# Priority for the weight sums and parts of the t2 and t3 products in all early pairs of a SwiGLU

## The chip, the cores and the metric

One core of one Trainium2 chip runs the whole program. The metric is device time in microseconds (us), the median of 3 runs. Matrix products run on TensorE (PE, with PEld for its weight loads), elementwise work on VectorE (DVE) and ScalarE (ACT), a little on GpSimd (POOL); SyncE (SP) issues nearly all DMAs.

## The reference, cut to what matters

Two request groups (512 and 256 tokens, handled as 768 columns) go through two layers. Each layer has a half SwiGLU, a mixer, and another half SwiGLU, so there are four SwiGLUs, which this text counts from 1 to 4:

```python
def swiglu(h, wg, wu, wd):
    return (jax.nn.silu(h @ wg) * (h @ wu)) @ wd

def even_layer(x, ...):
    x = x + 0.5 * swiglu(rmsnorm(x, f1_n), f1_g, f1_u, f1_d)
    x = x + mixer_ab(rmsnorm(x, mix_n), ...)
    x = x + 0.5 * swiglu(rmsnorm(x, f2_n), f2_g, f2_u, f2_d)
    return x
```

The odd layer has the same form with another mixer. D_MODEL is 1024, D_FF 2816, everything is float32.

## The kernel before, in words

**Precision.** An fp32 operand is split into a high part (rounded to a format TensorE multiplies fast) and a low remainder, and a product is three passes: high by high, low by high, high by low (`mm3`, L152). For weights, `wsplit` writes the high part `whi` with an ACT cast (L122) and the low part `wlo` with a DVE subtraction (L123).

**Seven products in place of eight.** The gate and up products of a SwiGLU are made by a Strassen-like scheme over 2 x 2 blocks: the columns' halves (384 each), the two halves of the 1024 rows, and two tiles of 128 hidden features. 22 tiles of hidden features make 11 pairs (`pair(p)`). Each pair and each of gate and up needs the products with the operands b11, b21, t2, t3, n4, t1 and b22. The products with t2, t3, t1 and b22 take sums of weight blocks, made on DVE at L727 (`sums`): s1 and s2 for t2, s3 for t3, s1 again for t1, and s4, which is formed in place over s2, for b22.

**Early pairs.** The first four pairs (`EARLY = 4`) start before the operands and the norm's scale are all there. They run b11 and b21 first, in an interleaved order (`ORDERS`), with their results copied by ACT out of PSUM (`p1`, L602), reload their weights, and then run `settle`: for t2, t3, n4, t1, b22, each for gate and up, the weights' parts (`parts`) are written one product ahead, and the first parts of the next pair are entered during the current one. In pair 0's `settle` PE also meets the matmuls that spread the norm's scale of the second half of the columns (`ps_aux<-diag,onesr`); what they read, `diag`, is made on DVE at the end of a chain of small 128x3 operations (L317 to L308). The products t1 and b22 accumulate in one PSUM bank: after t1 DVE adds the bank to u3 (`add`, L577), and only then may b22 go on in it.

**What sets the order.** PE's order is the order of the code. On the other engines a scheduler orders the instructions when the program is built, by the order of the code, dependences and its own estimates; inside `high_priority()` it takes an instruction earlier. On the chip each engine then takes its list in order. A weight load (512 KB, SP, `raw<-in_w`) waits for one of four buffers, that is, for the last reader of an older weight. Before the change one thing in `parts` had priority: t2's sums and parts, and of one pair alone, pair 0 in the first SwiGLU and pair 3 in the others (`urgent`, L484 and L548).

Of the kernel before, what the change touches and what calls it, by code (L numbers as in the profile page):

```python
# [44 lines left out]
EARLY = 4  # L45
# [10 lines left out]
class Trunk:  # L56
# [421 lines left out]
    def ffn(self, pre):  # L478
# [2 lines left out]
            self.fw = self.open("work", self.other(self.guards["comb"][1]))  # L481
        rt, scales = self.acc, self.scales
        mixed = bool(self.unfed)
        urgent = 0 if self.first else EARLY - 1  # L484
        hs = {}

        etile = self.etile
# [38 lines left out]
        def pair(p):  # L526
# [16 lines left out]
            def sums(n, name):  # L543
                return self.sums(a[n, 1, 1], a[n, 1, 2], a[n, 2, 1], a[n, 2, 2], s, n, name)

            def parts(n, b):
                name = {"t2": "s2", "t3": "s3", "t1": "s1", "b22": "s4"}.get(b)
                with self.tc.high_priority() if b == "t2" and p == urgent else nullcontext():  # L548
                    return self.wsplit(sums(n, name) if name else a[n, 2, 2], nc.vector)

            def product(n, w, b, key, start, st=None):
# [89 lines left out]
            def entry():  # L641
                load((0, 1))
                return parts("gate", "t2")

            def settle(st):

                todo = [(n, b) for b in ("t2", "t3", "n4", "t1", "b22") for n in names]
                key = {"t1": "Z", "b22": "Z"}
                for i, (n, b) in enumerate(todo):
                    now, st = st, None  # L650
                    if i + 1 < len(todo):
                        st = parts(*todo[i + 1])
                    elif p + 1 < EARLY and (p % 2 or not p):
                        entered[p + 1] = entries[p + 1]()
                    if b == "t2":
                        begin(n, e[n, "p1"])
                    product(n, None, b, key.get(b, "Y"), b == "t1", now)
                    if b in ("t2", "t3"):
                        keep(b.replace("t", "u"), "Y", n)
                    elif b == "n4":  # L660
                        next(steps, None)
                    else:
                        add("Z", n, "u3" if b == "t1" else "u2")
                    if n == "up":
                        if b == "n4":
                            hidden(1, 0, bank["Y", "gate"], bank["Y", "up"])
                        elif b == "t1":
                            hidden(1, 1, e["gate", "u3"], e["up", "u3"])
                        elif b == "b22":
                            hidden(0, 1, e["gate", "u2"], e["up", "u2"])  # L670
# [1135 lines left out]
```

## Time and profile before

| what | value |
|---|---|
| median of 3 runs | 2600.09 us (2599.57 to 2600.18) |
| the profiled execution, first to last instruction (its own time) | 2599.3 us |
| what lies around that span, against the median | 0.8 us |
| PE busy | 2557.6 us (98%), 15114 matmuls |
| DVE busy | 2250.6 us (87%), 4691 instructions |
| ACT busy | 1364.7 us (53%), 2869 instructions |

PE is nearly full, so the time is the sum of its matmuls plus its waits. A row of the waits view names who waited, for what, how long in total, how often, and the longest. A timeline row is start, duration, engine, line, operation, output and inputs, and, in brackets, the engine's idle time before it and what ended it. Buffer numbers are left out of names there. DVE and ACT overlap the end of one instruction with the next, so what one costs in a full queue is the distance of two starts, not its duration.

### The profile page before, as it was taken

The numbers are of one execution on the slowest core, as the hardware profiler recorded it, in microseconds if no ns is written. First come the engines' busy times: TensorE is split into PE (matmuls) and PEld (weight loads), VectorE is DVE, ScalarE is ACT, GpSimd is POOL, SyncE is SP. The second block draws the span as 40 slices with busy tenths as digits, with TensorE's granted clock in tenths as the row PEclk, the third lists the DMA queues.
The fourth block names the chain that finished last, engine by engine and source line by source line (L and its number), as shares of the span: only waits on it lengthen the run. The fifth ranks groups of instructions, "written<-read, shape, count | busy, mean of one in ns | idle before, by whom it ended". The sixth has DMA issues, their size and how long they took to land.

```text
span 2599.3 us, 41191 instructions
## 1 busy us (share of the span) xinstructions
PE 2557.6 (98%) x15114; PEld 2489.5 (96%) x15114; DVE 2250.6 (87%) x4691; ACT 1364.7 (53%) x2869; POOL 113.4 (4%) x191
## 2 busy tenths in 40 slices
PE   8999999999999999999999999999999999999998
PEld 8999999988899999999999999998898999999997
DVE  7998898889779989889999889886777699888897
ACT  7554454556656544445655445454545475444543
POOL 0000000000120000000000000001222210000000
PEclk9999999999999999999999999999999999999999
DMA  6333222421133322223222222242221332222222
GB/s 217 112 106 101 71 82 66 139 84 51 55 106 98 98 66 74 74 65 98 84 95 79 68 76 71 65 145 64 64 64 40 106 98 90 82 68 79 69 67 77
DMA packets 86202, 221.88 MB, mean 85 GB/s; under 512 B 20464, under 2 KB 33264, under 8 KB 86000
## 3 DMA queue, kind: packets, MB, share of 16 engines
q1 hardware_dynamic: 85712, 218.96, 26.9%
q8 instruction: 119, 1.95, 0.3%
q14 instruction: 83, 0.68, 0.1%
q10 hardware_dynamic: 288, 0.29, 0.0%
HBM read 209.78 MB, written 15.07 MB: 87 GB/s over the span
## 4 chain that ended last, share of the span: by engine, by line
PE 66%; DVE 5%; ACT 1%; issue 1%; DMA 1%; DVEq 0%; ACTq 0%; SPq 0%
PE ps_mm L152 40%; PE ps_aux L152 25%; PE ps_aux L156 1%; DVE wlo L123 1%; DMA raw<-in_w 1%; ACT p L1089 0%; DVE tmp L415 0%; DVE p L1099 0%; DVE p L1083 0%; DVE s L727 0%; DMA mf<-in_nmask 0%; DVE u L589 0%; DVE u L577 0%; DVE acc L235 0%; DVE tmp L393 0%
## 5 line engine op out<-in xcount | busy, mean ns | idle before, releaser
L122 ACT CAST whi<-s 128x512 fp32r<-128x512 f32 x496 | 304.9, 621 | 404.7 <-DVE s L727 178.6
L122 ACT CAST whi<-raw 128x512 fp32r<-128x512 f32 x504 | 305.4, 619 | 215.6 <-PE ps_mm L152 87.5
L123 DVE TENSOR_TENSOR wlo<-s,whi 128x512 fp32r<-128x512 f32 x496 | 338.3, 686 | 53.3 <-ACT whi L122 48.2
L123 DVE TENSOR_TENSOR wlo<-raw,whi 128x512 fp32r<-128x512 f32 x468 | 320.7, 693 | 15.2 <-ACT whi L122 11.3
L152 PE MATMUL ps_mm<-db,whi 128*128 128x384 f32 x864 | 219.3, 334 | 0.4 <-DVE sg L586 0.4
L152 PE MATMUL ps_aux<-dt,whi 128*128 128x384 f32 x864 | 219.2, 334 | 0.0
L152 PEld LDWEIGHTS ps_mm<-db,whi 128*128 128x128 f32 x864 | 155.9, 188 | 0.8 <-DVE sg L586 0.8
L152 PEld LDWEIGHTS ps_aux<-dt,whi 128*128 128x128 f32 x864 | 156.0, 188 | 0.0
L152 PE MATMUL ps_mm<-xh,whi 128*128 128x512 f32 (+1 forms) x416 | 146.2, 352 | 0.0
L152 PE MATMUL ps_aux<-dt,wlo 128*128 128x384 f32 x432 | 144.4, 334 | 1.4 <-DVE wlo L123 1.4
L152 PE MATMUL ps_mm<-db,wlo 128*128 128x384 f32 x432 | 144.3, 334 | 0.0
L152 PE MATMUL ps_mm<-xl,whi 128*128 128x512 f32 (+1 forms) x416 | 141.4, 340 | 0.0
L152 PE MATMUL ps_mm<-xh,wlo 128*128 128x512 f32 (+1 forms) x416 | 141.2, 339 | 0.0
L727 DVE TENSOR_TENSOR s<-raw 128x512 f32<-128x512 f32 x124 | 85.0, 687 | 20.9 <-DMA raw<-in_w 20.9
L577 DVE TENSOR_TENSOR u<-ps_aux,u 128x384 f32<-128x384 f32 x176 | 97.3, 553 | 5.6 <-PE ps_aux L152 5.2
L727 DVE TENSOR_TENSOR s<-raw,raw 128x512 f32<-128x512 f32 x124 | 84.2, 687 | 20.4 <-DMA raw<-in_w 20.2
L152 PE MATMUL ps_aux<-dh,whi 128*128 128x384 f32 x384 | 97.5, 334 | 0.0
L779 DVE TENSOR_TENSOR x<-ps_aux,x 128x384 f32<-128x384 f32 x160 | 84.9, 552 | 13.6 <-PE ps_aux L152 13.6
L1089 ACT ACTIVATE p<-p,st 128x256 f32<-128x256 f32 (+3 forms) x144 | 68.9, 480 | 49.4 <-DVE st L1087 49.3
L572 ACT COPY u<-ps_mm 128x384 f32<-128x384 f32 x176 | 83.5, 475 | 16.7 <-PE ps_mm L152 16.6
L779 DVE TENSOR_TENSOR x<-ps_mm,x 128x384 f32<-128x384 f32 x160 | 86.4, 552 | 5.8 <-PE ps_mm L152 5.5
L152 PEld LDWEIGHTS ps_mm<-xh,whi 128*128 128x128 f32 x416 | 79.8, 192 | 9.3 <-issue 0.9
(515 smaller groups left out, 8088.5 us busy)
## 6 DMA issues: line engine op xcount, KB each, us to landing
raw<-in_w SPq DMA_DIRECT2D x346, 512.0 KB, 3.7
xdm<-x SPq DMA_DIRECT2D x16, 384.0 KB, 2.4
x<-in_x SPq DMA_DIRECT2D x16, 192.0 KB, 4.6
tok<-in_xt SPq DMA_DIRECT2D x12, 256.0 KB, 5.2
xold<-xdm SPq DMA_DIRECT2D x8, 384.0 KB, 3.1
x<-xdm SPq DMA_DIRECT2D x8, 384.0 KB, 4.6
out_y<-y SPq DMA_DIRECT2D x8, 384.0 KB, 2.7
tab<-skew SPq DMA_DIRECT2D x8, 256.0 KB, 6.3
```

Of the source, the lines that this page charges most:

```text
L122: nc.scalar.copy(hi, src)
L123: (eng or nc.gpsimd).tensor_tensor(out=lo, in0=src, in1=hi.bitcast(F32), op=ALU.subtract)
L152: self.nc.tensor.matmul(out, lhsT=lhsT, rhs=rhs, start=start, stop=stop, **kw)
L156: self.nc.tensor.transpose(out, src, self.ident)
L572: nc.scalar.copy(e[n, out], bank[key, n])
L577: nc.vector.tensor_tensor(out=t, in0=bank[key, n], in1=t, op=ALU.add)
L727: f = lambda o, x, y, op: self.nc.vector.tensor_tensor(out=o, in0=x, in1=y, op=op)
L779: nc.vector.tensor_tensor(out=o, in0=ps, in1=o, op=ALU.add)
L1089: ins = nc.scalar.activation(outs[i], outs[i], AF.Exp, bias=nm[:, i : i + 1], accum_out=sm[:, i : i + 1])
```

## The change

`urgent` goes, and the sums and parts of t2 and of t3 get priority in each of the four early pairs, in each of the four SwiGLUs.

```diff
@@ -481,7 +481,6 @@
         rt, scales = self.acc, self.scales
         mixed = bool(self.unfed)
-        urgent = 0 if self.first else EARLY - 1
         hs = {}
@@ -545,7 +544,7 @@
             def parts(n, b):
                 name = {"t2": "s2", "t3": "s3", "t1": "s1", "b22": "s4"}.get(b)
-                with self.tc.high_priority() if b == "t2" and p == urgent else nullcontext():
+                with self.tc.high_priority() if b in ("t2", "t3") and p < EARLY else nullcontext():
                     return self.wsplit(sums(n, name) if name else a[n, 2, 2], nc.vector)
```

No instruction is added or removed. The order on PE and POOL stays; that on DVE, ACT and SP changes in the first 50 to 250 us of each SwiGLU and nowhere else. One line is gone, so the changed program's lines from L485 on are one lower (L727 is L726 there).

Place 1 is DVE in SwiGLU 2, pair 0, where the chain of the norm's scale ends in `diag`. wlo617 is the low part for t3, wlo618 and wlo620 are those for n4, wlo621 that for t1; t12l and t13l are low parts of the operand t1. Before:

```order
L295 CAST yh_9084<-sm_8914 128x3
L408 SCALAR_TENSOR_TENSOR t11l_8202<-tmp_8587,gains_99,t11h_8201 128x384
L296 TENSOR_TENSOR yl_9085<-sm_8914,yh_9084 128x3
L308 TENSOR_SCALAR diag_9088<-ident_84,yh_9084 128x128 x3
L123 TENSOR_TENSOR wlo617_9055<-s3_9052,whi617_9054 128x512
L123 TENSOR_TENSOR wlo618_9075<-raw115_8987,whi618_9074 128x512
L408 SCALAR_TENSOR_TENSOR t12l_8204<-tmp_8589,gains_99,t12h_8203 128x384
L123 TENSOR_TENSOR wlo620_9111<-raw117_8991,whi620_9110 128x512
L408 SCALAR_TENSOR_TENSOR t13l_8206<-tmp_8591,gains_99,t13h_8205 128x384
L123 TENSOR_TENSOR wlo621_9129<-s1_8993,whi621_9128 128x512
```

With the change:

```order
L123 TENSOR_TENSOR wlo618_9075<-raw115_8987,whi618_9074 128x512
L326 TENSOR_TENSOR sm_8914<-sm_8914 128x3
L408 SCALAR_TENSOR_TENSOR t12l_8204<-tmp_8589,gains_99,t12h_8203 128x384
L327 TENSOR_TENSOR sm_8914<-sm_8914 128x3
L123 TENSOR_TENSOR wlo620_9111<-raw117_8991,whi620_9110 128x512
L328 SCALAR_TENSOR_TENSOR sm_8914<-sm_8914 128x3
L408 SCALAR_TENSOR_TENSOR t13l_8206<-tmp_8591,gains_99,t13h_8205 128x384
L295 CAST yh_9084<-sm_8914 128x3
L123 TENSOR_TENSOR wlo621_9129<-s1_8993,whi621_9128 128x512
L296 TENSOR_TENSOR yl_9085<-sm_8914,yh_9084 128x3
L308 TENSOR_SCALAR diag_9088<-ident_84,yh_9084 128x128 x3
```

Six instructions that stood behind `diag` now stand ahead of it (the five here and wlo617), and none that stood ahead has gone behind. SwiGLU 4 shows the same six.

Place 2 is DVE in SwiGLU 2, end of pair 0 and start of pair 1. u3_9108 is the L577 addition of `up` that frees the bank for the b22 product of `up`; raw118 to raw121 are pair 1's weights. Before:

```order
L577 TENSOR_TENSOR u3_9072<-ps_aux623_9156,u3_9072 128x384
L727 TENSOR_TENSOR s1_9225<-raw119_9219 128x512
L586 TENSOR_TENSOR u3_9072<-u3_9072,acc_8239 128x384
L727 TENSOR_TENSOR s2_9227<-s1_9225,raw118_9217 128x512
L577 TENSOR_TENSOR u3_9108<-ps_aux625_9177,u3_9108 128x384
L727 TENSOR_TENSOR s1_9250<-raw121_9223 128x512
```

With the change:

```order
L576 TENSOR_TENSOR u3_9072<-ps_aux623_9156,u3_9072 128x384
L726 TENSOR_TENSOR s2_9227<-raw118_9217,s2_9227 128x512
L726 TENSOR_TENSOR s1_9250<-raw121_9223 128x512
L585 TENSOR_TENSOR u3_9072<-u3_9072,acc_8239 128x384
L726 TENSOR_TENSOR s2_9252<-s1_9250,raw120_9221 128x512
L726 TENSOR_TENSOR s3_9278<-raw118_9217,raw119_9219 128x512
L726 TENSOR_TENSOR s3_9301<-raw120_9221,raw121_9223 128x512
L123 TENSOR_TENSOR wlo628_9255<-s2_9252,whi628_9254 128x512
L123 TENSOR_TENSOR wlo630_9281<-s3_9278,whi630_9280 128x512
L123 TENSOR_TENSOR wlo632_9304<-s3_9301,whi632_9303 128x512
L576 TENSOR_TENSOR u3_9108<-ps_aux625_9177,u3_9108 128x384
```

Nine more instructions stand ahead of u3_9108 than before, all 128x512: the eight here with L726 and L123, and wlo627 a few rows higher. They are the sums and parts of pair 1's t2 and t3 and, with the second s2_9227, the sum for its b22.

Place 3 is ACT in SwiGLU 3, where the result of the b11 product of `up`, pair 3, is copied out of bank ps_mm998 (p1_14318), before the b21 product may go on in it. whi1004 reads the sum s2_14386, which needs pair 0's last weight load. Before:

```order
L594 COPY ps_mm1007_14414<-p1_14013 128x384
L602 COPY p1_14318<-ps_mm998_14278 128x384
L122 CAST whi1004_14388<-s2_14386 128x512
L587 ACTIVATE sg_14320<-sg_14320 128x384
L587 ACTIVATE sg_14362<-sg_14362 128x384
```

With the change:

```order
L593 COPY ps_mm1007_14414<-p1_14013 128x384
L122 CAST whi1004_14388<-s2_14386 128x512
L601 COPY p1_14318<-ps_mm998_14278 128x384
L122 CAST whi1006_14410<-s3_14408 128x512
L586 ACTIVATE sg_14320<-sg_14320 128x384
```

The cast whi1004 has moved from behind the copy to ahead of it.

## Rows read from the trace of the kernel before

**Rows 1.** The page, part 1: busy time, share of the span, instructions.
```profile
PE 2557.6 (98%) x15114; PEld 2489.5 (96%) x15114; DVE 2250.6 (87%) x4691; ACT 1364.7 (53%) x2869; POOL 113.4 (4%) x191
```

**Rows 2.** PE's waits, 45 to 160 us (SwiGLU 1): who, for what: us, times, longest.
```profile
PE ps_mm L152 <- ACT whi L122: 4.1, 2, 2.2
PE ps_mm L152 <- DVE wlo L123: 2.3, 4, 0.8
```

**Rows 3.** PE's waits, 785 to 860 us (SwiGLU 2).
```profile
PE ps_mm L152 <- DVE wlo L123: 2.2, 4, 0.8
PE ps_mm L152 <- ACT whi L122: 1.2, 2, 0.9
```

**Rows 4.** PE's waits, 2112 to 2190 us (SwiGLU 4), those for high parts.
```profile
PE ps_mm L152 <- ACT whi L122: 1.2, 2, 1.0
```

**Rows 5.** Windows in SwiGLU 2, 3, 4: length, busy PE, PEld, DVE, ACT, POOL, clock, DMA.
```profile
785.00:809.90 24.90, 23.36 (x134) 22.39 (x133) 24.90 (x64) 18.30 (x42) 0.00 (x0) 1.00 0.30 85
785.00:831.00 46.00, 43.66 (x249) 42.17 (x248) 45.77 (x102) 27.80 (x61) 0.00 (x0) 1.00 0.30 92
1278.00:1310.00 32.00, 32.00 (x186) 31.51 (x185) 28.70 (x67) 17.30 (x37) 0.00 (x0) 1.00 0.29 100
2112.00:2158.00 46.00, 43.67 (x248) 42.17 (x247) 45.76 (x102) 27.79 (x61) 0.00 (x0) 1.00 0.31 92
```

**Rows 6.** PE's timeline in SwiGLU 2, pair 0.
```profile
803.46 0.44 PE L152 MATMUL ps_mm<-t20h,whi 128*128 128x384 f32 x1 [0.95 <-ACT whi L122]
809.92 0.51 PE L152 MATMUL ps_aux<-diag,onesr 128*128 128x384 f32 x2
821.71 0.33 PE L152 MATMUL ps_aux<-b220h,whi 128*128 128x384 f32 x1
```

**Rows 7.** DVE's timeline in SwiGLU 2, pair 0.
```profile
807.57 0.68 DVE L308 TENSOR_SCALAR diag<-ident,yh 128x128 fp32r<-128x128 f32 x3
808.16 0.69 DVE L123 TENSOR_TENSOR wlo<-s,whi 128x512 fp32r<-128x512 f32 x1
808.76 0.69 DVE L123 TENSOR_TENSOR wlo<-raw,whi 128x512 fp32r<-128x512 f32 x1
820.05 0.56 DVE L577 TENSOR_TENSOR u<-ps_aux,u 128x384 f32<-128x384 f32 x1
```

**Rows 8.** DVE's waits over the whole span.
```profile
DVE s L727 <- DMA raw<-in_w: 41.1, 59, 2.2
```

**Rows 9.** Windows after a long PE wait (the first of five at 0.50), and after short ones.
```profile
56.88:60.29 3.41, 3.41 (x13) 3.41 (x12) 3.41 (x10) 2.09 (x6) 0.00 (x0) 0.50 0.00 0
804.50:808.00 3.50, 3.24 (x17) 2.92 (x18) 3.50 (x13) 2.15 (x5) 0.00 (x0) 1.00 0.00 0
```

**Rows 10.** ACT's timeline in SwiGLU 3: the copy of place 3 and the cast behind it.
```profile
1288.15 0.48 ACT L602 COPY p<-ps_mm 128x384 f32<-128x384 f32 x1 [1.27 <-PE ps_mm L152]
1289.34 0.62 ACT L122 CAST whi<-s 128x512 fp32r<-128x512 f32 x1 [0.70 <-DVE s L727]
```

**Rows 11.** DVE's timeline in SwiGLU 3: `diag`.
```profile
1298.76 0.68 DVE L308 TENSOR_SCALAR diag<-ident,yh 128x128 fp32r<-128x128 f32 x3
```

**Rows 12.** PE's timeline in SwiGLU 3: the b21 product of place 3, and the spread.
```profile
1290.04 0.33 PE L152 MATMUL ps_mm<-b210h,whi 128*128 128x384 f32 x1
...
1299.49 0.45 PE L152 MATMUL ps_aux<-diag,onesr 128*128 128x384 f32 x1
```

**Rows 13.** PE's timeline in SwiGLU 1, pair 1: t2 and b22.
```profile
78.73 0.44 PE L152 MATMUL ps_mm<-t20h,whi 128*128 128x384 f32 x1 [1.88 <-ACT whi L122]
95.60 0.33 PE L152 MATMUL ps_aux<-b220h,whi 128*128 128x384 f32 x1
```

**Rows 14.** PE's waits, 96 to 160 us (SwiGLU 1).
```profile
PE ps_mm L152 <- DVE wlo L123: 1.2, 2, 0.8
```

**Rows 15.** DVE's timeline in SwiGLU 1, pair 1: the L577 addition of `gate`.
```profile
93.72 0.56 DVE L577 TENSOR_TENSOR u<-ps_aux,u 128x384 f32<-128x384 f32 x1
```

## The prediction

> **What bounds the kernel now.** I read the page's shares of busy time first: PE is busy 98% of the span, DVE 87%, ACT 53% [rows 1]. PE's order of work is the same in both kernels, so the time can change only by PE's waits and by the clock at which its matmuls run. Next I read the waits view, in the stretches where the orders differ. In SwiGLU 1 PE waits 4.1 + 2.3 = 6.4 us for the high and low parts of weights [rows 2], in SwiGLU 2 2.2 + 1.2 = 3.4 us [rows 3], in SwiGLU 4 the same 3.4 us (1.2 of it for high parts [rows 4], and its window of 46.00 us holds 43.67 us of busy PE against 43.66 [rows 5]); in SwiGLU 3 it is busy in the whole window of 32.00 us and waits for no part [rows 5]. Together 13.2 us, 0.5% of the time, can be won from waits for t2 and t3. Last I asked what DVE could spare. In the early pairs of SwiGLU 2 it is busy 45.77 of 46.00 us, in those of SwiGLU 4 45.76 [rows 5]. DVE has no idle time there, so a part made earlier makes something else later by the same time. The prediction is therefore about what gets later, and how much slack that has.
>
> One price is needed throughout: an instruction of 128x512 on DVE costs 0.60 us in a full queue (starts at 807.57, 808.16, 808.76 [rows 7]), though each lasts 0.69.
>
> A second is that of a sum that stands in the queue before its weights have landed: DVE waited 41.1 us in 59 waits of that kind, 0.70 each [rows 8]. For several sums that wait for loads one behind the other I take 1.0 in all (0.5 to 2.1, three full waits).
>
> A third is the clock. After long waits of PE the granted clock stood at 0.50, the lower level of 1.2 GHz, for 3.41 us: the stretch at 56.88 came just behind the wait of 2.2 us in SwiGLU 1 [rows 2, 9]. There are five such stretches in the trace. Behind the waits at 803 to 804 us, the longest 0.95 [rows 6], the clock stayed at 1.00 [rows 9]. A stretch at 0.50 holds 13 matmuls where 17 stood in 3.50 us at full clock [rows 9], so it costs some 0.7; it can cost no more than half of itself, 1.7. I take 1.0 for one, bounds 0 to 1.7.
>
> **SwiGLU 2.** *Place 1, the spread of the scale.* `diag` ends at 807.57 + 0.68 = 808.25 [rows 7], and PE comes to its matmul at 809.92 without waiting [rows 6]: 1.67 us of slack. Six instructions of about 0.60 now stand ahead, 3.6 us, and pair 1's sums, taken earlier, meet loads that have not landed, 0.6 of the 1.0 above. `diag` then ends at 812.45, and PE starts 0.05 later, at 812.5: 2.6 late. Up to 809.9 it was busy 23.36 of 24.90 us [rows 5]; without those 1.54 us of waits for t2 and t3 it arrives at 808.4, so it would stand for 4.1 us.
>
> *Place 2, the bank of b22.* The L577 addition of `up` starts at 820.05, ends at 820.61 [rows 7], and PE's b22 product of `up` starts at 821.71 [rows 6]: slack 1.1. Nine more instructions of 128x512 now stand ahead, 9 x 0.60 = 5.4; the waits for loads add 1.0, and 0.5 (0 to 1) where DVE waits for PE, which is late itself since place 1. The addition starts at 820.05 + 6.9 = 826.95, ends at 827.5, and b22 starts then: 5.8 late. This contains place 1's 2.6, it does not add to it, because the same DVE queue carries both: PE stands about 3.2 us more here. Behind the addition is the rest of DVE's queue; the low parts for b22 of `up` stood ahead already, so nothing more is late for the same product.
>
> *Pairs 1 and 2.* The t2 waits behind 809.9 are 3.4 - 1.54 = 1.8 us, and go. The same additions stand at the ends of these pairs, again behind sums and parts of the next pair; I take 0.8 for them (0, the queue having been drained while PE waited, to 3.2, as in pair 0). One stretch at half clock behind the wait of place 2: 1.0. Sum: 5.8 - 1.8 + 0.8 + 1.0 = **+5.8 us** (bounds +3 to +10).
>
> **SwiGLU 4.** Its order has the same six and nine instructions, its waits and its DVE load are the same [rows 4, 5], so it gets **+5.8**.
>
> **SwiGLU 3.** It had no such wait, so nothing can be won, unless its other small waits move. *Place 3, ACT's copy:* it starts at 1288.15 and the cast behind it at 1289.34, after 0.70 us of waiting for DVE's sum [rows 10]. PE's b21 product starts at 1290.04 [rows 12]. With the cast ahead, the copy runs after it: 1289.34 + 0.62 + 0.48 = 1290.4, and 0.6 later with the sum's load wait: PE is 1.0 late. *`diag`:* it ends at 1298.76 + 0.68 = 1299.44 [rows 11], and PE's spread starts at 1299.49 [rows 12], so there is no slack. Two more sums stand ahead, 1.2, and a load wait, 0.7: 1.9 late, with the 1.0 inside it. The additions before b22 in pair 1 add 0.6 (0 to 1.8). **+2.5** (0 to 5).
>
> **SwiGLU 1.** Pair 0's waits for t3, of which the longest is 2.2 [rows 2], go, as does the half clock at 56.88, and those of 1.2 behind 96 us [rows 14] go too; the wait of 1.88 for pair 1's t2 [rows 13] stays, because its sums keep their place in DVE's order. At the end of pair 1 the addition of `gate` starts at 93.72 [rows 15] and b22 at 95.60 [rows 13], slack 1.3. Eight more sums and parts stand ahead and one has gone behind, 8 x 0.60 - 0.47 = 4.3; DVE comes there earlier by 1.5 (0 to 2.5: what PE gains in pair 0 is 2.2 and a little more, and I take some two thirds of it). So b22 starts at 93.72 + 4.3 - 1.5 + 0.56 = 97.1, 1.5 late against before whatever was won ahead of it, since PE's gain in pair 0 ends in this wait. Half clock behind it 1.0, and the 1.2 gone: 1.5 + 1.0 - 1.2 = **+1.3** (-2 to +4).
>
> **The sum.** 1.3 + 5.8 + 2.5 + 5.8 = 15.4. The profiled execution, span 2599.3 and 0.8 around it, 2600.1, is the median itself, so no shift is needed: 2600.1 + 15.4 = **2615.5 us**. DMA issues of SP are moved too: weight loads wait for the last reader of a buffer. Earlier sums free buffers earlier; the queue is not full in these stretches (its DMA share is 0.30 [rows 5]), so I cost that at nothing beyond the load waits above; if it turns out otherwise, loads come earlier and the 1.0 in each SwiGLU shrinks to 0.5.
>
> **A rule against this.** The rows above show that what t2 waits for stands in a queue without idle time, where something else with a slack of 1.1 to 1.7 us stands behind it. The Trainium skill, Perfetto Trace Analysis, section Optimization Strategy, tells one to find the gaps of the engine that bounds the kernel, see which instruction ends each, and make that dependency start sooner; by this the change is right, and the sum would be the 13.2 us of waits, a gain. The page says nothing of what is pushed back.
>
> **Rivals.**
>
> *The waits only move.* PE waits 13.2 us now because DVE has too much to do in the early pairs; the same instructions in another order have the same sum, so PE gets its 13.2 us back at t2 and t3 and loses them at `diag` and the additions. For it: DVE's load does not change. Against: t2's waits are small pieces that each end one instruction, while at place 2 nine instructions count at once, and SwiGLU 3 has nothing to get back. Time 2600 +-3. Chance 0.08.
>
> *The slack covers it: faster.* The six and nine instructions are not extra time ahead of `diag` and the additions if DVE comes to these places ahead of its old time, because sums that waited for loads or for PE were done before. Place 1 decides: with DVE there 2.6 us ahead, or six instructions at 0.28 in place of 0.60, 1.67 us of slack are enough. Then the 13.2 us go, 2586.9, and with the stretches at half clock behind the two waits of 1.9 to 2.2 us in SwiGLU 1 gone up to 3.4 more, 2583.5. Against: DVE is busy 45.77 of 46.00 us [rows 5], so there is no earlier time to move to. Chance 0.05.
>
> *Heavier.* Every long wait is followed by half clock, two stretches in each of SwiGLU 2 and 4 and one in 3 at 1.7, and the additions of pairs 1 and 2 wait as in pair 0: per SwiGLU 2.4 + 2.4 more (3.2 for 0.8; 3.4 for 1.0), in 3 2.5 more, 15.4 + 9.6 + 2.5 = 27.5 at most; half of the excess gives 2621.6, the whole 2627.6. Chance 0.12.
>
> **How the numbers follow.** The forecast as worked out has 0.75, heavier 0.12, moved waits 0.08, faster 0.05. The bounds of single terms lie wide, but several of them are independent; the range 2606 to 2624 takes the lower ends of SwiGLU 1 and 3 (-3.3, -2.5) with 1.5 off each of the other two, and on the upper side half of the heavier case; it leaves out the two light rivals (0.13) and the worst part of the heavy one. 0.2%, about what a measurement tells from no change, is 5.2 us, so "same" ends at 2605.3: faster 0.05, same 0.08, slower 0.87.
>
> **What would show it right or wrong.** Right: in PE's waits of SwiGLU 2 and 4 those for `whi` and `wlo` are nearly gone, and two others stand there, one of about 4 us for `diag` (DVE, L307) and one of about 3 for `u` (L576) at b22 of `up`, pair 0, which comes about 5.8 us later than before, counted from 785; half clock behind it. In SwiGLU 3 PE waits for ACT's copy and for `diag`; in SwiGLU 1 b22 of pair 1 waits for an addition. Wrong: `diag` within 1.7 us of its old time in SwiGLU 2 would refute place 1; b22 of `up` without a wait, place 2; waits that sum to 13 us in all, as before, would be the first rival, and a total below 5 us the second.

## The result, and the profile after

The changed kernel takes 2613.89 us (median of 5 runs, 2611.16 to 2614.50) against 2600.18 us for the kernel before in the same comparison: a ratio of 1.0049, 95% interval 1.0038 to 1.0059, so 10 to 15 us slower. The forecast was 2615.5 us, range 2606 to 2624. The profiled execution took 2611.59 us with a span of 2609.8, at the lower end of its runs; against the span of 2599.3 before it is 10.5 us longer, and the accounts below are made against that. All runs on record take 1.7 to 2.1 us more than their span, so the kernel before was profiled in an execution of about 2601.1 us, 0.9 above its median; the 0.8 us around that span, by which the prediction took it for the median itself, is a misreading. The changed kernel was profiled 2.3 us below its median. Together this is what 10.5 lacks of the 13.7 us between the medians.

The page's busy times are what they were [rows 1], within 5 us each:

```profile
PE 2557.7 (98%) x15114; PEld 2490.9 (95%) x15114; DVE 2255.1 (86%) x4691; ACT 1366.7 (52%) x2869; POOL 112.4 (4%) x191
```

PE's waits in SwiGLU 2, 785 to 860 us of the changed kernel. All rows of [rows 3] are gone, and two others stand there (the prediction's L307 is this L308, since only the lines from L485 on have moved):

```profile
PE ps_aux L152 <- DVE diag L308: 4.4, 1, 4.4
PE ps_aux L152 <- DVE u L576: 2.6, 2, 2.4
```

SwiGLU 4, 2112 to 2190 us, the twin:

```profile
PE ps_aux L152 <- DVE diag L308: 4.5, 1, 4.5
PE ps_aux L152 <- DVE u L576: 2.6, 2, 2.4
```

SwiGLU 3, 1278 to 1420 us, where there was no wait for a part:

```profile
PE ps_aux L152 <- DVE u L576: 1.6, 1, 1.6
PE ps_aux L152 <- DVE diag L308: 1.4, 1, 1.4
```

SwiGLU 1, 45 to 160 us, the answer to [rows 2]. These waits sum to 7.2 us, where 6.4 stood before, and yet PE leaves this stretch earlier; why is told under SwiGLU 1 below:

```profile
PE ps_aux L152 <- DVE u L576: 2.7, 1, 2.7
PE ps_mm L152 <- DVE wlo L123: 1.3, 2, 1.0
PE ps_aux L152 <- ACT whi L122: 1.1, 1, 1.1
PE ps_mm L152 <- ACT whi L122: 1.1, 1, 1.1
PE ps_aux L152 <- DVE b223l L209: 0.8, 1, 0.8
PE ps_aux L152 <- DVE wlo L123: 0.2, 1, 0.2
```

The two places in PE's timeline of SwiGLU 2. In [rows 6] the same matmuls start at 809.92 and 821.71 without a wait:

```profile
807.44 0.44 PE L152 MATMUL ps_aux<-diag,onesr 128*128 128x384 f32 x1 [4.42 <-DVE diag L308]
823.67 0.41 PE L152 MATMUL ps_aux<-b220h,whi 128*128 128x384 f32 x1 [2.38 <-DVE u L576]
```

And DVE's queue between the two additions of place 2: behind the first L576 row stand eight instructions of 128x512 with L726 and L123 (the rows show how many they hold as x2 and x3) before the addition at 822.97 for which PE waits. Before the change it was two, as the order of place 2 shows, and the addition started at 820.05 [rows 7]:

```profile
817.22 0.55 DVE L576 TENSOR_TENSOR u<-ps_aux,u 128x384 f32<-128x384 f32 x1
817.69 0.68 DVE L726 TENSOR_TENSOR s<-raw,s 128x512 f32<-128x512 f32 x1
818.29 0.68 DVE L726 TENSOR_TENSOR s<-raw 128x512 f32<-128x512 f32 x1
818.89 0.55 DVE L585 TENSOR_TENSOR u<-u,acc 128x384 f32<-128x384 f32 x1
819.36 0.68 DVE L726 TENSOR_TENSOR s<-s,raw 128x512 f32<-128x512 f32 x1
819.96 1.29 DVE L726 TENSOR_TENSOR s<-raw,raw 128x512 f32<-128x512 f32 x2
821.17 1.89 DVE L123 TENSOR_TENSOR wlo<-s,whi 128x512 fp32r<-128x512 f32 x3
822.97 1.01 DVE L576 TENSOR_TENSOR u<-ps_aux,u 128x384 f32<-128x384 f32 x2
```

**PE's delay by stretch.** PE's order is the same in all kernels here, so the start of the same matmul can be subtracted between two traces. The marks are 1.25, 282.6, 797.8, 858.5, 1281.0, 1368.7, 2125.0 and 2190.9 us in the trace before; the table has the change of the delay from mark to mark, in us, and the delay of the last matmul, which holds the stretches between as well.

| kernel (one profiled execution) | SwiGLU 1 | 282.6 to 797.8 | SwiGLU 2 | SwiGLU 3 | SwiGLU 4 | last matmul |
|---|---|---|---|---|---|---|
| forecast | +1.3 | 0 | +5.8 | +2.5 | +5.8 | +15.4 |
| the change | -2.3 | -2.4 | +6.0 | +2.5 | +5.5 | +9.7 |
| e1 first only | -2.2 | -1.5 | 0.0 | -0.8 | -0.1 | -1.6 |
| e2 rest only | -1.0 | -0.5 | +5.0 | +1.8 | +6.1 | +11.2 |
| e3 t2 only | -0.9 | +1.2 | +1.9 | +2.6 | +2.1 | +7.8 |
| e4 t3 only | -0.8 | 0.0 | -0.1 | -0.7 | +1.3 | +0.2 |
| e5 additions first | -3.5 | 0.0 | +2.3 | +0.5 | +1.3 | +2.9 |
| e6 without pair 1 | -2.5 | +0.1 | +2.3 | +2.3 | +3.8 | +7.1 |
| e7 diag first | -2.6 | -1.2 | 0.0 | -1.2 | +0.9 | -1.5 |
| e8 small step | -2.9 | +1.1 | 0.0 | -0.9 | +0.1 | -2.0 |
| e9 GpSimd | -1.3 | +1.6 | +6.3 | -1.3 | +7.3 | +17.1 |
| e10 GpSimd on e8 | -2.8 | +4.6 | +5.8 | -0.9 | +8.0 | +28.3 |
| e11 GpSimd on e7 | -2.5 | +0.5 | +3.4 | -0.2 | +6.6 | +13.5 |
| e12 ACT | -0.7 | -2.0 | -2.8 | -0.1 | -1.7 | -7.7 |

The column 282.6 to 797.8 is mostly the mixer, which no edit touches; it moves by -2.4 to +4.6 between kernels, and 28 executions of the kernel before in one comparison lay between 2596.5 and 2603.9 us. The column SwiGLU 1 holds the start of the program too: up to 45 us, e1 is 1.7 us ahead of the kernel before and the change 0.2, with the same order there. One execution's differences of 1 us mean little, so verdicts below go by the ratios.

### The profile page after: what moved, and what is told of

The parts are those of the page before. It is cut to its first block, busy times and chain, and to the rows that moved or that the text cites. A ratio compares the mean times of both kernels' runs of the same rounds, so it can differ in the third digit from the quotient of the medians.

```text
span 2609.8 us, 41221 instructions
## 1 busy us (share of the span) xinstructions
PE 2557.7 (98%) x15114; PEld 2490.9 (95%) x15114; DVE 2255.1 (86%) x4691; ACT 1366.7 (52%) x2869; POOL 112.4 (4%) x191
## 3 DMA queue, kind: packets, MB, share of 16 engines
q8 instruction: 119, 1.95, 0.3%
## 4 chain that ended last, share of the span: by engine, by line
PE 64%; DVE 6%; DMA 1%; issue 1%; ACT 1%; DVEq 0%; ACTq 0%; SPq 0%
PE ps_mm L152 39%; PE ps_aux L152 25%; DMA raw<-in_w 1%; DVE wlo L123 1%; PE ps_aux L156 1%; DVE s L726 1%; ACT p L1088 0%; DVE p L1098 0%; DVE tmp L415 0%; DVE p L1082 0%; DMA mf<-in_nmask 0%; DVE v L587 0%; DVE sg L585 0%; DVE sg L588 0%; DVE acc L235 0%
## 5 line engine op out<-in xcount | busy, mean ns | idle before, releaser
L123 DVE TENSOR_TENSOR wlo<-s,whi 128x512 fp32r<-128x512 f32 x496 | 335.3, 684 | 51.8 <-ACT whi L122 46.5
L123 DVE TENSOR_TENSOR wlo<-raw,whi 128x512 fp32r<-128x512 f32 x468 | 320.6, 692 | 17.9 <-ACT whi L122 14.2
L726 DVE TENSOR_TENSOR s<-raw 128x512 f32<-128x512 f32 x124 | 85.0, 686 | 26.0 <-DMA raw<-in_w 25.9
L576 DVE TENSOR_TENSOR u<-ps_aux,u 128x384 f32<-128x384 f32 x176 | 96.7, 551 | 6.8 <-PE ps_aux L152 6.5
L726 DVE TENSOR_TENSOR s<-raw,raw 128x512 f32<-128x512 f32 x124 | 82.7, 684 | 19.1 <-DMA raw<-in_w 19.0
L778 DVE TENSOR_TENSOR x<-ps_aux,x 128x384 f32<-128x384 f32 x160 | 84.6, 550 | 13.2 <-PE ps_aux L152 13.2
L586 ACT ACTIVATE u<-u 128x384 f32<-128x384 f32 x88 | 46.2, 525 | 82.9 <-DVE u L585 82.8
L586 ACT ACTIVATE sg<-sg 128x384 f32<-128x384 f32 x88 | 46.3, 526 | 82.5 <-DVE sg L585 81.9
```

The source lines that it names most:

```text
L123: (eng or nc.gpsimd).tensor_tensor(out=lo, in0=src, in1=hi.bitcast(F32), op=ALU.subtract)
L576: nc.vector.tensor_tensor(out=t, in0=bank[key, n], in1=t, op=ALU.add)
L586: nc.scalar.activation(t, t, AF.Silu)
L726: f = lambda o, x, y, op: self.nc.vector.tensor_tensor(out=o, in0=x, in1=y, op=op)
L778: nc.vector.tensor_tensor(out=o, in0=ps, in1=o, op=ALU.add)
```

## The experiments

**e1 and e2: the change in SwiGLU 1 alone, and in the others alone.**

```diff
+        opening = bool(self.first)
 ...
-                with self.tc.high_priority() if b in ("t2", "t3") and p < EARLY else nullcontext():
+                with self.tc.high_priority() if b in ("t2", "t3") and p < EARLY and opening or b == "t2" and p == EARLY - 1 and not opening else nullcontext():
```

(e2: `opening` and `not opening` exchanged, with t2 of `p == 0` in SwiGLU 1.)

> The change in SwiGLU 1 alone, the rule of before in the other three. Theory (the loss is made in SwiGLU 2 to 4): PE gains what the profile of the changed kernel shows in SwiGLU 1, 2.3 us up to its last wait for t2 and another 1.1 at 290 us, so 2596.7 (2595.5 to 2598.5). Rival, the forecast's term for SwiGLU 1 of +1.3: 2601.4. Rival, waits only move: 2600 with nothing gained.

> The change in SwiGLU 2, 3 and 4, the rule of before in SwiGLU 1. Theory: the drift of PE against before is +5.6 in SwiGLU 2, +2.5 in 3 and +6.4 in 4, together 14.5, so 2614.6 (2612 to 2618); waits of 4.4 us for diag and 2.4 us for u at b22 of up in SwiGLU 2 and 4. Rival, waits only move: 2600 to 2603. Rival, the loss starts from what SwiGLU 1 does to the loads behind it: SwiGLU 2 then shows no wait of 4 us for diag.

Measured: e1 ratio 0.9990 (0.9981 to 0.9999), 2.6 us faster; e2 1.0057 (1.0044 to 1.0071), 14.8 us slower, with the waits of 4.3 and 2.4 us in SwiGLU 2. Together 12.2 us, against 12.7 us for the change (0.0049 of 2600). So the parts add up, the whole loss is made in SwiGLU 2 to 4, and SwiGLU 1 gains. The forecast's term for 2 to 4, 14.1, holds; that for SwiGLU 1, +1.3, falls. Of the versions here that compute the same, e1 alone is faster than both kernels, and its interval reaches almost to 1. Traces bear the gain out: from 45 to 160 us PE gets 2.2 us ahead in the change and 2.1 to 2.3 in e6, e7 and e11, which have its order there; in e1's own trace, which has a stretch at half clock there, it is 0.6.

**e3 and e4: t2 alone, and t3 alone, in all early pairs.**

```diff
-                with self.tc.high_priority() if b in ("t2", "t3") and p < EARLY else nullcontext():
+                with self.tc.high_priority() if b == "t2" and p < EARLY else nullcontext():
```

(e4: `b == "t3"`.)

> Priority for t2 alone, in all early pairs of all SwiGLUs; t3 has none. Theory (an instruction newly ahead of diag or of the additions is what costs): nothing new stands ahead of diag in SwiGLU 2 and 4 and the additions there have one instruction less ahead, so the t2 waits of 3.1 us go in each of the two with nothing in return; SwiGLU 3 keeps its two sums ahead of diag and its cast ahead of the copy, +2; SwiGLU 1 -1.5 (its t3 waits stay). Sum -5.7: 2594.4 (2592 to 2598), and no wait for diag over 1 us in SwiGLU 2. Rival (any priority in pairs 1 and 2 costs, by loads not landed and by the queue's sum): 2605 or more.

> Priority for t3 alone, in all early pairs; t2 has none, not even in the one pair that had it before. Theory: four instructions are newly ahead of diag in SwiGLU 2 and 4, 2.4 us and 0.6 for loads against 1.67 of slack, so a wait for diag of 1.3 to 2.5 us, and one only ahead of the additions, 0.6 against 1.1, so none there; the t2 waits stay. +2 in each of SwiGLU 2 and 4, +0.5 in 3, -1 in 1: 2603.6 (2600 to 2607). Rival (t3 carries the whole loss): 2612 or more.

Measured: e3 1.0028 (1.0017 to 1.0038), 7.3 us slower where 5.7 faster was expected. Its waits in SwiGLU 2, 785 to 860 us:

```profile
PE ps_mm L152 <- ACT whi L122: 2.3, 2, 1.1
PE ps_mm L152 <- DVE wlo L123: 1.9, 5, 0.6
PE ps_aux L152 <- DVE u L576: 0.2, 1, 0.2
```

No wait for `diag` came, as expected, but the sum for parts rose from 3.4 to 4.2 us: in its timeline they now stand at t3, two products later (1.11 us at 806.05, 1.14 at 852.73). t2's parts were made at the cost of t3's. This is the first rival's mechanism, waits that only move, in miniature. The table has the loss as +1.9 and +2.1 in SwiGLU 2 and 4, where 3.1 each was to be won, and +2.6 in SwiGLU 3, where +2 was expected.

e4: 0.9997 (0.9988 to 1.0006), no difference. The four instructions ahead of `diag` cost PE 0.4 us there and not 1.3 or more. `diag` ends at 809.69, with e4's 0.88 us of lead at this place 810.57 in before's time: 2.3 late, so without the 0.6 for loads, and 0.65 over the slack of 1.67. The other 0.2 is PE, which t2's parts, now behind t3's, held longer just before (1.00 us at 804.20 where it was 0.34). Neither half of the change makes the two long waits: each alone puts none to four instructions ahead of these places, both together six and nine. But t2 alone loses more than half of what the change loses, in other waits.

**e5: place 2 undone.** The additions before and after b22 get priority too.

```diff
             def add(key, n, other):
                 t = e[n, other]
-                nc.vector.tensor_tensor(out=t, in0=bank[key, n], in1=t, op=ALU.add)
+                with self.tc.high_priority() if early and key == "Z" else nullcontext():
+                    nc.vector.tensor_tensor(out=t, in0=bank[key, n], in1=t, op=ALU.add)
```

> The change, with priority also for the additions to u2 and u3 before and after b22 in early pairs. In DVE's order this takes six of the nine instructions away from ahead of the addition of place 2 in SwiGLU 2 (three stay), but leaves ten ahead of it in SwiGLU 4, and leaves six ahead of diag in both: a control inside one run. Theory (the wait is the queue ahead of the addition): in SwiGLU 2 the 2.4 us wait for u at b22 goes and the 4.4 us one for diag stays; in SwiGLU 4 both stay; in SwiGLU 1, where one in place of seven stands ahead, the 2.7 us wait goes. Changed kernel 2613.9 - 2.4 - 2.0 = 2609.5 (2607 to 2612). Rival (DVE's sum decides and waits only move): PE reaches b22 with no less delay and another wait of 2 us stands behind it; 2613 to 2615.

Measured: 1.0020 (1.0011 to 1.0029), 5.2 us slower than before, so 7.5 us of the change's loss are gone, more than the 4.4 expected. One sentence of the expectation was a misreading: the ten instructions in SwiGLU 4 stand ahead of the multiplication by the scale that has the same output, not of the addition; ahead of the addition three stand, as in SwiGLU 2. There was no control, and both SwiGLUs should lose the wait for `u`. Both do, and SwiGLU 1 loses its wait of 2.7, as expected. SwiGLU 2, 785 to 860 us (SwiGLU 4, 2112 to 2190, has the same row):

```profile
PE ps_aux L152 <- DVE diag L308: 4.4, 1, 4.4
```

With place 2 gone, PE's delay is +2.3 in SwiGLU 2 in place of +6.0: place 2 was worth 3.7 us beyond place 1.

**e6: pair 1 without priority in SwiGLU 2 to 4.**

```diff
+        opening = bool(self.first)
 ...
-                with self.tc.high_priority() if b in ("t2", "t3") and p < EARLY else nullcontext():
+                with self.tc.high_priority() if b in ("t2", "t3") and p < EARLY and (opening or p != 1) else nullcontext():
```

> The change without priority for pair 1 in SwiGLU 2, 3 and 4 (SwiGLU 1 as changed). Six still stand ahead of diag in SwiGLU 2 and 4, but three in place of nine ahead of place 2's addition, and none new ahead of diag in SwiGLU 3. Theory: the waits of 4.4 us for diag stay, those of 2.4 us for u go, the t2 waits of pair 1 (0.8 each) return, SwiGLU 3's wait of 1.4 us for diag goes: 2613.9 - 2 x 1.6 - 1.3 = 2609.4 (2607 to 2612). Rival (pair 1's early sums made the whole loss, place 1 too): 2600.

Measured: 1.0028 (1.0017 to 1.0040), 7.3 us slower than before, which on the scale of 2600.1 is 2607.4, at the lower edge of what was expected. The 4.4 us wait for `diag` stays in SwiGLU 2 and 4 and the 2.4 us for `u` is gone: place 2 comes from pair 1's parts, place 1 from pair 0's. SwiGLU 3 was a miss: the wait for `diag` falls from 1.4 to 0.2, but one for `u` rises from 1.6 to 2.1, and its delay stays at +2.3.

**e7: place 1 undone too.** The norm's chain and `diag` get a higher priority than the parts.

```diff
-            with self.tc.high_priority():
+            with self.tc.high_priority(1000000):
                 y = self.norm_tok(self.acc, c0, c1)
         yield d1
-        with self.tc.high_priority():
+        with self.tc.high_priority(1000000):
             self.r[h] = self.spread(self.early[h]) if self.tok else self.norm_spread(y)
```

> The change, with the norm's chain of small operations and diag given a far higher priority than the weights' parts in SwiGLU 2 to 4. In DVE's order diag then stands six places ahead of where it stood before the change and the additions of place 2 three to four ahead; the parts of t2 and t3 are still earlier than before, by 8 and 13 places in pair 0. Theory (what stands behind t2 and t3 is the loss): no wait over 1 us for diag or u in SwiGLU 2 and 4, -1 in each; SwiGLU 3 +0.5 (its cast stays ahead of the copy); SwiGLU 1 -3.4. 2596 (2592 to 2600). Rival (DVE's sum decides, waits only move): waits for parts of n4, t1 or the next pair take the place, 2605 or more.

Measured: 1.0004 (0.9995 to 1.0012). The whole loss is gone with two lines that change the order alone: what stands ahead of `diag` and, since the scheduler then places the rest otherwise, ahead of the additions. But the 4 us below the kernel before, which the theory expected, did not come. SwiGLU 2, 785 to 860 us:

```profile
PE ps_aux L152 <- DVE b223l L209: 1.6, 1, 1.6
PE ps_mm L152 <- DVE wlo L123: 1.0, 2, 0.6
PE ps_mm L152 <- ACT u L571: 0.8, 1, 0.8
PE ps_mm L152 <- ACT whi L122: 0.3, 1, 0.3
```

3.7 us of waits, as many as the 3.4 before, and in SwiGLU 4 5.6, for other things: operands of b22, ACT's copies. What t2 and t3 gain, others pay.

**e8: a smaller step.** Priority of 50 places in the code's order in place of the unbounded one.

```diff
-                with self.tc.high_priority() if b in ("t2", "t3") and p < EARLY else nullcontext():
+                with self.tc.high_priority(50) if b in ("t2", "t3") and p < EARLY else nullcontext():
```

> The change with a priority of 50 places in the code's order in place of the unbounded one, for the same parts in the same pairs. In DVE's order the low parts for t2 and t3 of pair 0 are 9 and 8 places earlier than before the change, diag one earlier, the additions of place 2 three earlier; in SwiGLU 3 nothing new stands ahead of the copy and of diag; in SwiGLU 1 two in place of eight are newly ahead of the addition. Theory: the t2 and t3 waits go in part (-2 in each of SwiGLU 2 and 4, -2.5 in 1, 0 in 3) with no new wait for diag or u over 0.5 us: 2593.6 (2590 to 2598), faster than both. Rival (DVE is full, so each early part makes a later one late): 2599 to 2603.

Measured: 1.0009 (1.0000 to 1.0018), the rival's 2599 to 2603 and not the theory's 2593.6. No long wait for `diag` or `u` came, as expected, but smaller ones did, 2.7 us in SwiGLU 2 (the one for `u` is for ACT's copy):

```profile
PE ps_mm L152 <- ACT u L571: 1.2, 1, 1.2
PE ps_aux L152 <- DVE b223l L209: 0.6, 1, 0.6
PE ps_mm L152 <- DVE wlo L123: 0.5, 1, 0.5
PE ps_aux L152 <- ACT diag L306: 0.4, 1, 0.4
```

In SwiGLU 2 and 4 the delay changes by 0.0 and +0.1. Both e7 and e8 keep the gain of SwiGLU 1 in their traces (-2.6 and -2.9) and are not faster by their ratios; their profiled executions lie 0.9 and 2.0 us below their medians, so part of this is the choice of the execution, and the rest stays open.

**e9 to e12: is it DVE's sum?** e7 and e8 suggest that in SwiGLU 2 and 4 no order gives anything, because DVE is full. Then less work on DVE must. e9 gives GpSimd the low parts for n4 of the early pairs of SwiGLU 2 and 4, on the kernel before; e10 does it on e8, e11 on e7. e12, on the kernel before, leaves these low parts out: ACT writes a copy of the weights in their place, so neither DVE nor GpSimd works there, and what comes of n4 is not the product.

```diff
-                    return self.wsplit(sums(n, name) if name else a[n, 2, 2], nc.vector)
+                    return self.wsplit(sums(n, name) if name else a[n, 2, 2], nc.gpsimd if early and mixed and b == "n4" else nc.vector)
```

(e12: `nc.scalar` for `nc.gpsimd` there, and in `wsplit`:)

```diff
-        (eng or nc.gpsimd).tensor_tensor(out=lo, in0=src, in1=hi.bitcast(F32), op=ALU.subtract)
+        if eng is nc.scalar:
+            nc.scalar.copy(lo, src)
+        else:
+            (eng or nc.gpsimd).tensor_tensor(out=lo, in0=src, in1=hi.bitcast(F32), op=ALU.subtract)
```

> The kernel before, with the low part for n4 (128x512, eight in each of SwiGLU 2 and 4's early pairs) made by GpSimd, which is empty there, in place of DVE: 8 x 0.60 = 4.8 us less on DVE in each. Theory (in SwiGLU 2 and 4 DVE's sum sets how much PE waits in the early pairs, whatever the order): the waits for t2 behind pair 0's n4, 1.8 us in each, go; those of pair 0 stay: 2600.1 - 3.6 = 2596.5 (2594 to 2599). Rival (the order alone sets the waits, or GpSimd's 1.3 us per part comes too late or slows DVE): 2599 to 2603.

> The change with the priority of 50 places, and n4's low parts of the early pairs of SwiGLU 2 and 4 on GpSimd. Theory (DVE's sum): what the small step left as moved waits in SwiGLU 2 and 4, 2.5 to 3 us each, falls to 1 each, and SwiGLU 1 keeps its -2.8: 2600.1 - 2.8 - 2 x 2 = 2593.3 (2590 to 2598). Rival (waits move on to ACT's copies of u and to b22's parts all the same): 2598 to 2602.

> The change with the norm's chain and diag ahead of the weights' parts, and n4's low parts of the early pairs of SwiGLU 2 and 4 on GpSimd. Theory (DVE's sum): the waits of 3.7 and 5.8 us that were left in SwiGLU 2 and 4 with diag ahead fall by half, SwiGLU 1 keeps its -3.4, SwiGLU 3 its -1: 2600.1 - 3.4 - 1 - 2 x 2 = 2591.7 (2589 to 2598). Rival (waits move on all the same): 2598 to 2602.

> The kernel before, with the n4 low parts of the early pairs of SwiGLU 2 and 4 left out as parts: ACT writes a copy of the weights' sum in their place, so what is computed for n4 there is not the remainder, and the time is that of eight instructions less on DVE and eight more on ACT in each, with GpSimd idle. The order on DVE is that of the run with GpSimd. Theory (DVE's sum, and GpSimd's parts of 3.5 us were what spoiled the test before): the 1.8 us of waits behind pair 0's n4 go in each, and no wait of 3.7 to 4.6 us for u comes: 2600.1 - 3.6 = 2596.5 (2594 to 2599). Rival (the order that the scheduler makes of it, sums ahead of their loads and of the additions, is what costs, not GpSimd): 2608 to 2620, with the wait for u at b22 of pair 1 in place.

Measured: e9 1.0064 (1.0052 to 1.0077), e10 1.0095 (1.0082 to 1.0109), e11 1.0035 (1.0021 to 1.0049): all three clearly slower, outside every range given. GpSimd is not free. Its rows and DVE's in e9, SwiGLU 2, around 830 us:

```profile
829.70 5.51 POOL L123 TENSOR_TENSOR wlo<-raw,whi 128x512 fp32r<-128x512 f32 x1 [17.92 <-DVE db L209]
```

```profile
834.12 1.51 DVE L496 TENSOR_TENSOR sg<-u,sg 128x384 f32<-128x384 f32 x1
835.55 1.77 DVE L123 TENSOR_TENSOR wlo<-s,whi 128x512 fp32r<-128x512 f32 x1
841.49 0.69 DVE L727 TENSOR_TENSOR s<-raw 128x512 f32<-128x512 f32 x1 [4.17 <-DMA raw<-in_w]
```

This GpSimd part takes 5.51 us beside a busy DVE, where the same kind took 1.29 us at 776 in the trace before, and DVE's instructions then take 1.51 and 1.77 in place of 0.55 and 0.68. It is the longest of the eight in SwiGLU 2; the others take 1.29 to 1.95 us (the 3.5 us in e12's expectation is a row of two). SwiGLU 4 shows the same. GpSimd's part is the last reader of a weight's buffer, and the waits of SyncE's DMA queue show what this holds (826 to 842 us; the second row is the weight loads behind GpSimd):

```profile
SPq L107 <- DVE s L727: 10.4, 1, 10.4
SPq L107 <- POOL wlo L123: 9.3, 2, 8.1
```

The next load comes late, DVE waits 4.17 us for it at the head of its queue, and PE 3.67 us for an addition behind. The Trainium skill, SBUF — State Buffer, section Who interferes with whom, says that a VectorE instruction with two inputs in SBUF contends with a GpSimd instruction that reads SBUF; these rows agree, and give its price here.

e12 takes GpSimd out of it: 0.9987 (0.9978 to 0.9996), 3.4 us faster, as the theory said (3.6). In SwiGLU 2, 785 to 860 us, what is left is the waits of pair 0, which stand ahead of the first n4:

```profile
PE ps_mm L155 <- ACT whi L122: 0.9, 1, 0.9
PE ps_mm L155 <- DVE wlo L126: 0.6, 2, 0.3
```

1.5 us in place of 3.4, with t2 and t3 given no more priority than before. So the waits in these pairs hang on DVE's sum, and GpSimd's slow parts were what spoiled e9, both with one reservation: that e12's weight buffers come free earlier may have helped by itself, and was not told apart. Whether e10's and e11's order would gain with ACT in GpSimd's place was not tried, nor was a form of e12 that computes n4's remainder.

## Why the prediction was right, point by point

**SwiGLU 2 and 4 right, +5.8 each forecast, +6.0 and +5.5 measured.** Place 1: PE enters the two places 4.70 us earlier than before (a matmul of the b21 product ahead of pair 0's t2 starts at 793.14, before at 797.84). `diag` ends at 807.4, which is 812.1 in before's time, that is, with the 4.70 added; the forecast had 812.45. PE stood 4.42 us for it, forecast 4.1. The six instructions cost what was said, 3.8 us against 3.6; the 0.6 for loads did not come, as no wait of DVE for a load stands ahead of `diag`. Place 2: b22 at 823.67 is 828.4, forecast 827.5; PE stood 2.38, forecast 3.2. e5, e6 and e7 show that the loss starts at these two places: place 1 alone leaves +2.3 in SwiGLU 2, both gone 0.0.

The parts of the 6.9 us at place 2 were mis-sized, and offset each other. DVE's waits in the changed kernel up to the addition of place 2, 785 to 823.4 us:

```profile
DVE sg L585 <- PE ps_mm L152: 0.8, 1, 0.8
DVE v L587 <- PE ps_mm L152: 0.5, 1, 0.5
DVE s L726 <- DMA raw<-in_w: 0.2, 1, 0.2
```

Waits for loads were 0.2 (forecast 1.0), for PE 0.76 + 0.46 = 1.2 (forecast 0.5). With nine instructions at 0.60 that makes 6.8; by PE's lead the addition came 7.6 late, and the other 0.8 is not traced. PE was late by its wait for `diag`, and by the clock: the granted clock fell to 0.50 behind both waits of SwiGLU 2 and for twice as long behind the first of SwiGLU 4, where the forecast paid for one stretch in each. Windows at 0.50 in SwiGLU 2 (two) and SwiGLU 4 (one, twice as long):

```profile
807.76:811.17 3.41, 3.41 (x11) 3.30 (x11) 3.23 (x7) 1.20 (x4) 0.00 (x0) 0.50 0.47 137
824.83:828.24 3.41, 3.41 (x12) 3.41 (x11) 2.48 (x6) 1.14 (x2) 0.00 (x0) 0.50 0.35 80
2142.38:2149.21 6.83, 5.96 (x18) 5.82 (x19) 5.31 (x13) 2.46 (x6) 0.00 (x0) 0.50 0.56 191
```

11 and 12 matmuls, where full clock has 77 in 13.08 us at the same place before, 20 in 3.41: a stretch costs some 1.5 us, near the upper bound of 1.7 and not the 1.0 taken. The forecast's 0.7 came of a window with waits in it: its 17 matmuls in 3.50 us had 3.24 of busy PE [rows 9].

So the number owes something to luck. In SwiGLU 2 b22 came 0.9 later than forecast and the stretch behind it cost 0.6 more; in return the t2 waits of pairs 1 and 2 gave back 2.8 where 1.8 was counted, and the additions there cost 0.5 and not 0.8. In SwiGLU 4 b22 came 7.7 late, with the longer stretch inside that and none behind. That a wait gives back more than its row says shows in SwiGLU 1 of the trace before:

```profile
103.31 0.44 PE L152 MATMUL ps_mm<-t20h,wlo 128*128 128x384 f32 x1 [0.79 <-DVE wlo L123]
```

Without the wait this matmul and the next come 1.06 us earlier against those ahead. The row counts idle time alone; in a full stream matmuls start 0.17 us apart though each lasts 0.33, and around a wait this overlap is lost as well.

**SwiGLU 3 right in sum, by other parts.** Place 3 cost nothing: ACT's copy now runs at 1290.84, and PE's b21 starts behind it at 1291.36, which is 1290.04 [rows 12] plus the 1.32 us of delay that PE brought along. The cast and the copy:

```profile
1290.31 0.62 ACT L122 CAST whi<-s 128x512 fp32r<-128x512 f32 x1 [2.73 <-DVE s L726]
1290.84 0.47 ACT L601 COPY p<-ps_mm 128x384 f32<-128x384 f32 x1
```

`diag` cost 1.4 where 1.9 was said, and the addition before b22 1.6 where 0.6 (0 to 1.8) was; 0.6 came back behind it, where a wait of 0.4 for `sg` had stood.

**SwiGLU 1 wrong: +1.3 forecast, -2.3 measured, and e1 is 2.6 us faster by its ratio.** The step that failed is "DVE comes there earlier by 1.5 (0 to 2.5)". The addition of `gate` at the end of pair 1 starts at 94.67, not at 93.72 + 4.3 - 1.5 = 96.5: DVE came 3.35 us earlier.

```profile
94.67 1.01 DVE L576 TENSOR_TENSOR u<-ps_aux,u 128x384 f32<-128x384 f32 x2
```

The forecast took two thirds of what PE gains in pair 0 for this, and did not read DVE's idle time here. Windows from 45 to 96 us, the kernel before and then the change:

```profile
45.00:96.00 51.00, 45.86 (x242) 44.58 (x241) 48.00 (x105) 29.34 (x63) 0.00 (x0) 0.93 0.39 111
```

```profile
45.00:96.00 51.00, 43.72 (x242) 41.33 (x241) 50.77 (x110) 29.19 (x62) 0.00 (x0) 1.00 0.38 111
```

DVE (the third busy time) had 3.0 us of idle time there and 0.2 with the change, so the early parts filled 2.8 of it; in SwiGLU 2 and 4 it had 0.2 to begin with [rows 5]. That the idle time is the cause is read from these rows; no run tested it. This term is 1.8 us of the 3.6 between forecast and trace. The half clock behind b22 of pair 1 (1.0) did not come in this execution (in e1's it did), and 0.8 more went from the later waits than the 1.2 counted.

Where the gain lies in time is not where one would look. The same two rows have a mean clock of 0.93 and 1.00: the stretch at 56.88 [rows 9] is gone, and so is a second one, which came 2 us after the wait of 1.88 for pair 1's t2 [rows 13]:

```profile
80.77:84.18 3.41, 3.41 (x13) 3.41 (x12) 2.96 (x6) 2.38 (x5) 0.00 (x0) 0.50 0.23 38
```

But what these two and the early waits give, some 7 us, is taken back by new waits, for parts of n4 and b22, for an operand of b22 and for the addition, up to b22 of pair 1, which starts at 95.27 against 95.60. The 2.1 us that stay are won behind it, where the waits of [rows 14] are gone.

**Outside the early pairs.** 1.1 us went at 288 us, a wait for `wlo` that was longer before. The rest of the -2.4 between 282.6 and 797.8 is the clock: the trace before has a stretch at 0.50 at 701.99 us that the change's has not, and PE gains 1.5 us over it. Such stretches differ between kernels that do not touch the mixer, so this is not the change's; it may be part of why the profiled execution shows 10.5 us and the medians 13.7. No profile of a longer execution of the change was taken.

**The rivals.** "Slack covers it" fell: DVE was not ahead, but only SwiGLU 1 had idle time to move into, and there it did win. "Waits only move" was wrong for the change, which lost, but it is the right description of what is left when the two places are mended (e7, e8) or when t2 alone goes first (e3): of the 13.2 us of waits, the 6.8 in SwiGLU 2 and 4 could be won by none of the orders tried. Of the heavier case the clock came, two stretches' worth in each of SwiGLU 2 and 4, but not the waits at the ends of pairs 1 and 2 (0.2 us in each of the two SwiGLUs, where 3.2 was its price), nor the stretch in SwiGLU 3. Of the rule that the prediction named (start sooner what the bounding engine waits for), the runs show where it held: SwiGLU 1, with idle time on DVE and waits to win, gained 2.6 us; SwiGLU 2 and 4, with waits but no idle time, lost. SwiGLU 3 lost too, though DVE was busy for only 28.70 of 32.00 us [rows 5]: it had no wait to win, and `diag` had no slack.

## What to carry to other kernels

Before giving work priority on an engine that takes its list in order, read that engine's idle time in each stretch separately: where there was some, early work filled it (SwiGLU 1); where there was none, each instruction moved forward delayed what it passed by its price, 0.60 us here. List what is passed, and compare the sum with the slack of what PE awaits there; six and nine passed instructions against 1.67 and 1.1 us of slack carried the forecast of 5.8 us per SwiGLU, while its terms for loads, for PE and for the clock were off and offset each other. Where the engine was full, no order that was tried helped; less work on it did (e12), and moving the work to GpSimd, which contends with it, did not.

## What the runs showed of the hardware that was not expected

A GpSimd subtraction of 128x512 took up to 5.51 us beside a full DVE (1.29 to 1.95 for the other seven in SwiGLU 2) against 1.29 us at 776 in the trace before, where DVE was almost idle, and single DVE instructions beside it 1.51 and 1.77 us against 0.55 and 0.68 (e9). And the granted clock stayed at 0.50 for 6.83 us, not 3.41, behind the 4.5 us wait of SwiGLU 4, twice as long as each of the five stretches of the trace before that the forecast counted.
